# An encoder trunk whose start loads lie in one array: norm weights, first weight chunk and x side by side, and the small loads on SyncE's queue

## The chip, the cores and the metric

The kernel runs on one core of a Trainium2 chip. The metric is the device time of one execution in microseconds. The kernel before takes 593.35 us (median of 3 runs, 592.43 to 595.54). The engines are named as in the profile: PE (TensorE), DVE (VectorE), ACT (ScalarE), POOL (GpSimd) and SP (SyncE, which here only issues transfers).

## The reference, cut to what matters

Two residual layers over x of 256 tokens and 1024 features, all in float32:

```
h = x
for layer in range(2):
    hn = rms_norm(h, norm_mix_g[layer])
    if layer == 0:                       # grouped-query attention (A) beside dilated attention (B)
        qa, ka, va, qb, kb, vb = split(hn @ ab_w_in[0])
        qa, ka = rope(rms_norm(qa, a_q_norm_g)), rope(rms_norm(ka, a_k_norm_g))
        mix = concat(attention_A(qa, ka, va), attention_B(qb, kb, vb, rel_bias)) @ ab_w_out[0]
    else:                                # latent attention
        mix = mla_attention(hn, c_w_down, c_q_norm_g, c_kv_norm_g, c_w_uq, c_w_ukv) @ c_w_out
    h = h + mix
    hn = rms_norm(h, norm_mlp_g[layer])
    h = h + square(relu(hn @ mlp_w1[layer])) @ mlp_w2[layer]
return rms_norm(h, final_norm_g)
```

## The kernel before, in words

**Weights as a stream.** All weights lie in one array `wall`, cut into chunks of 128 rows by 2048 columns (1 MB each) in the order of their use. Chunks 0 and 1 (`qA`) make the queries of mixer A, chunk 2 (`kvA`) its keys and values, chunks 3 and 4 (`qkB` 0 and 1) the first half of the queries and of the keys of mixer B, chunks 5 and 6 their second half. `load` (L204) brings a chunk into one of three buffers `raw`; `split_piece` (L212) splits a quarter of it (later a half) into a rounded part `whi` (a copy on ACT, L222) and the remainder `wlo` (a subtraction on DVE, L223). When the last quarter of chunk i is split, `load(i + 3)` is given to SP (L225). Every product is three matmuls (`mm3`, L260): high by high (L263), high by low (L264), low by high (L265).

**The start.** PE runs 9 matmuls on zeros (L656). Chunk 0 comes in four quarters, each followed by rows of the transposed x (`xT`); the norm weights `g` (35 columns) come between. Then come chunk 1 in two halves, chunk 2 and the table `kc` with the identity, all issued by SP in this order. POOL issues three small loads: `gaq` (64 KB, one row of 512 bytes given to all 128 partitions, L645), `oh` (66 KB, L647) and `rb` (1 KB, L649). For each of the eight row blocks kk of x, `split_piece` prepares the weights, ACT scales xT by the norm weights and rounds it (hT, L663), DVE makes the remainder (L664), and PE does 6 matmuls of 512 columns. The code up to L677 is under `manual_schedule`: it stands in each engine's program as written.

**What follows.** 48 matmuls of 256 columns with chunk 2 (acckv), then 48 with chunk 3 and 48 with chunk 4 into the banks `s` (`qk_b(0)`, L781). Beside them `mixer_a` (L716) prepares mixer A: squares of the queries and keys on ACT (L720, L721), sums on DVE; the mean square of x (`mean_square`, L321: four squares of `xh` on ACT, L326); on POOL the tables `tab` and a chain of small operations that ends in `rs0`, the norm's factor by token (`rsqrt`, L307, L319); on DVE the rotation of the queries (`rope_a`, L696, result `qr`, last step L706), which PE then transposes (L752). `row_scales` (L332) multiplies the identity by `rs0` on DVE (`dg`, L336) for two more matmuls (L337). The scores of the first head (L847) close this stage.

**What sets the order.** From kvA on, a scheduler at build time decides the order of the instructions in each engine's program, from costs and arrival times that it assumes; the order of the code is only its input. Each engine then executes its own program strictly in that order. An instruction that waits holds up all that stand behind it on its engine.

Of the kernel before, what the change touches and what calls it, by code (L numbers as in the profile page):

```python
# [11 lines left out]
F32 = mybir.dt.float32  # L12
# [25 lines left out]
G_MIX, G_MLP, G_CQ, G_CKV = 0, 16, 32, 34  # L38
N_G = 35
R_AQ, R_AK, R_FIN = 0, 64, 128  # L40
N_R = 128 + D
# [4 lines left out]
def shape_constants():  # L46
    """Rotary tables, the relative-position buckets and the branch counts: of the shapes alone."""
    f = np.float32
# [44 lines left out]
def weight_chunks():  # L93
    """The order in which the weights stream in: (name, columns used)."""
    order = [("qA", 0), ("qA", 1), ("kvA", 0)]
    order += [("qkB", i) for i in range(4)] + [("vB", 0), ("vB", 1)]
    order += [("outA", i) for i in range(4)]
    for l in range(2):
        if l == 1:
            order += [("down", 0), ("down", 1), ("uq", 0), ("uq", 1), ("ukv", 0)]  # L100
            order += [("outC", i) for i in range(4)]
        for u in range(17):
            if u < 16:
                order.append((f"w1_{l}", u))
            if u > 0:
                order.append((f"w2_{l}", u - 1))
    return order
# [11 lines left out]
def pack_weights(ab_w_in, ab_w_out, c_w_down, c_w_uq, c_w_ukv, c_w_out, mlp_w1, mlp_w2):  # L119
    """All weights in the order of their use, each chunk as 128 partition rows."""  # L120
    win, wout = ab_w_in[0], ab_w_out[0]
# [44 lines left out]
@with_exitstack  # L166
def encoder(ctx: ExitStack, tc: tile.TileContext, x, xt, wall, gcol, grow, const, onehot, relb, out):
    nc = tc.nc
# [19 lines left out]
    def o_bank():  # L188
        return psum("o", 2)
# [9 lines left out]

# [1 line left out]
    raws, parts, done = {}, {}, set()  # L201
# [10 lines left out]
    def split_piece():  # L212
        """The next quarter of a chunk as two parts; of a chunk of the MLPs, the next half."""
        i, q = divmod(at["piece"], 4)
        n = 2 if i >= 5 else 1
        at["piece"] += n
        if q % 2 == 0:
            parts[i, q // 2] = [wp.tile([P, CW // 2], F32R, name=z, tag=z, bufs=W_BUFS) for z in ("whi", "wlo")]
        hi, lo = parts[i, q // 2]
        raw = raws[i][:, 512 * q:512 * (q + n)]  # L220
        s = slice(512 * (q % 2), 512 * (q % 2 + n))
        nc.scalar.copy(hi[:, s], raw)  # L222
        nc.vector.tensor_tensor(lo[:, s], raw, hi[:, s].bitcast(F32), op=OP.subtract)  # L223
        if q + n == 4:
            load(i + RAW_BUFS)  # L225
# [10 lines left out]
    def quarter(n=2):  # L236
        """A quarter of a chunk has been used."""
        at["quarter"] += 1
        pump(n)

    def take(name, j, n, whole=True):
        """A chunk of n row blocks: its operands by row block and columns."""
        i = at["take"]
        assert ORDER[i] == (name, j), (ORDER[i], name, j)
        at["take"] += 1
        while whole and at["piece"] < 4 * i + 4:
            split_piece()

        def operand(k, c=slice(None)):
            half, kk = divmod(k, n // 2)  # L250
            return tuple(z.rearrange("p (k c) -> p k c", k=n // 2)[:, kk, c] for z in parts[i, half])

        return i, operand
# [3 lines left out]
    def cols(i, n=P):  # L257
        return slice(i * n, i * n + n)

    def mm3(out, a, b, first, last):  # L260
        """out += a.T @ b, of operands that are each a sum of two parts."""
        (ah, al), (bh, bl) = a, b
        nc.tensor.matmul(out, ah, bh, start=first, stop=False)  # L263
        nc.tensor.matmul(out, ah, bl, start=False, stop=False)  # L264
        return nc.tensor.matmul(out, al, bh, start=False, stop=last)  # L265
# [6 lines left out]

# [1 line left out]
    g = cp.tile([P, N_G], F32, name="g")  # L274
# [4 lines left out]
    nc.vector.memset(idle, 0.0)  # L279
    xT = ap.tile([P, KT, S], F32, name="xT", tag="OT0")  # L280
    xt_v = xt.rearrange("(k p) t -> p k t", p=P)

    def load_x(a, b):
        nc.sync.dma_start(xT[:, a:b], xt_v[:, a:b])

    raws[0] = wp.tile([P, CW], F32, name="raw", tag="raw", bufs=RAW_BUFS)
    for a, b in ((0, 1), (1, 2), (2, 4), (4, 8)):
        for q in range(a, min(b, 4)):
            nc.sync.dma_start(raws[0][:, cols(q, 512)], wall[0, :, cols(q, 512)])
        load_x(a, b)  # L290
        if a == 0:
            nc.sync.dma_start(g, gcol)
    load(1, 2)
    load(2)
    kc = cp.tile([P, N_K], F32, name="kc")
    xh = cp.tile([P, NT, D], F32, name="xh")
    nc.sync.dma_start(kc, const)
    ident, flip = kc[:, K_ID:K_ID + P], kc[:, K_FLIP:K_FLIP + P]
    junk = cp.tile([P, 512], BF16, name="junk")
# [7 lines left out]
    def rsqrt(u, n, dst):  # L307
        """u ** -0.5, with one Newton step behind the power."""
        y, z = (small(16)[:, :n] for _ in range(2))
# [11 lines left out]
    def mean_square(name):  # L321
        """mean(h * h) + eps, a column for each token block."""
        part, u = small(4), cp.tile([P, NT], F32, name=f"u{name}")
        for t in range(NT):
            for c in range(2):
                nc.scalar.activation(junk, xh[:, t, cols(c, 512)], AF.Square,  # L326
                                     accum_out=part[:, 2 * c + t:2 * c + t + 1])
        nc.gpsimd.tensor_tensor(u, part[:, 0:2], part[:, 2:4], op=OP.add)
        nc.gpsimd.tensor_scalar(u, u, 1.0 / D, EPS, op0=OP.mult, op1=OP.add)
        return u  # L330

    def row_scales(bank, which, columns):  # L332
        """Values by token, spread over all partitions with the tokens along the row."""
        for t in range(NT):
# [3 lines left out]

# [1 line left out]
    def attention(heads, fill, dst):  # L340
# [34 lines left out]
        def values(j):  # L375
            """The weighted values of a pair of heads, side by side in the array."""
            ob = o_bank()
# [34 lines left out]
    def scaled_softmax(scale, nscale):  # L412
        """exp(scale * (s - max)) and its sums, the scale by query."""
        nb = {}
# [21 lines left out]
    def turn(c, t, gbase):  # L436
        """Half a token block of the residual stream, transposed, gained and split."""
        with tc.high_priority():
# [12 lines left out]
    class Later:  # L451
        """The turn of the last group, given out while the next one is computed."""
        todo = None
# [170 lines left out]

# [1 line left out]
    with tc.tile_pool(name="l0", bufs=1) as lp:  # L626
# [17 lines left out]

        nc.gpsimd.dma_start(gaq, bass.AP(tensor=grow.tensor, offset=grow.offset, ap=[[0, P], [1, P]]))  # L645
        oh = sp.tile([P, 512], F32, name="oh", tag="prob", bufs=3)
        nc.gpsimd.dma_start(oh[:NUM_BUCKETS + 1, :], onehot)  # L647
        nc.vector.memset(rb, 1.0)
        nc.gpsimd.dma_start(rb[:NUM_BUCKETS, :], relb)  # L649

        # q, then k and v, of mixer A
        acc = [mm_bank() for _ in range(NT)]
        with tc.manual_schedule():
# [3 lines left out]
            for j in range(2):  # L657
                i, w = take("qA", j, 4, whole=False)
                for k in range(4):
                    kk = 4 * j + k  # L660
                    gc = g[:, G_MIX + kk:G_MIX + kk + 1]
                    split_piece()
                    nc.scalar.activation(hT[0][:, kk], xT[:, kk], AF.Copy, scale=gc)  # L663
                    nc.vector.scalar_tensor_tensor(hT[1][:, kk], xT[:, kk], gc, hT[0][:, kk].bitcast(F32),  # L664
                                                   op0=OP.mult, op1=OP.subtract)
# [4 lines left out]
                if j == 0:  # L670
                    nc.sync.dma_start(xh, x.rearrange("(t p) d -> p t d", p=P))
            lines = o_bank()
            nc.tensor.matmul(lines[:HB, :], rb, oh[:NUM_BUCKETS + 1, :], start=True, stop=True)
# [16 lines left out]
        def load_bias(j):  # L690
            """rel_bias by distance, with the branch counts; query rows run backwards."""
            bias[j] = lp.tile([P, 2, 3 * P], F32, name="bias", tag="bias", bufs=2)
# [15 lines left out]
        def stack(dst, src, col):  # L708
            """Rows of two heads, each as its high part beside its low part in the other rows."""
            for s in range(2):  # L710
# [211 lines left out]

# [1 line left out]
    with tc.tile_pool(name="l1", bufs=1) as lp:  # L924
# [194 lines left out]
```

## Time and profile before

| what | before |
|---|---|
| runs, median (lowest to highest) | 593.35 us (592.43 to 595.54) |
| span of the profiled execution | 591.9 us |
| PE busy | 578.0 us (98%) |
| DVE, ACT, POOL busy | 364.7, 324.1, 35.0 us |
| first matmul on data | 6.21 us after the span's start |
| weights and inputs read | 95.05 MB |

The profiled execution has no time of its own beside its span; the span is 1.45 us below the median of the runs, and what lies around it is taken as these 1.45 us. PE is busy nearly all the time, so that time can be won or lost where PE stands idle or runs at the lower of its two clocks: at the start, in the stage up to 60 us, and at the end.

### The profile page before, as it was taken

What the parts mean: (1) busy time and instruction counts of PE and PEld (TensorE: products, weight loads), DVE (VectorE), ACT (ScalarE), POOL (GpSimd) and SP (SyncE); (2) the same over time, 40 slices, a digit from 0 to 9 for tenths busy, and PEclk for the clock granted to TensorE, in tenths of its full rate; (3) what the DMA queues carried; (4) which work ended last, traced back from release to release, by engine and by line L of the source; (5) the groups of instructions that cost most, each with busy time, mean ns of one, the idle gap of its engine ahead of it and who ended that gap; (6) DMA issues with size and microseconds to landing.
All of it is one profiled execution on the core that took longest, in us unless ns stands there. A gap on an engine that the chain in (4) does not pass through costs nothing.

```text
span 591.9 us, 8924 instructions
## 1 busy us (share of the span) xinstructions
PE 578.0 (98%) x3553; PEld 493.9 (83%) x3553; DVE 364.7 (62%) x583; ACT 324.1 (55%) x550; POOL 35.0 (6%) x70
## 2 busy tenths in 40 slices
PE   7989999999999999999999999999999999999994
PEld 3889665689998998898889987779899889989984
DVE  4888776586545546555468888757555645555425
ACT  5768875564444444435447498836444444544414
POOL 1480000000000000000002200000000000000003
PEclk9989999999999999999999999999999999999998
DMA  8955133135454555545544323146454554554201
GB/s 277 406 200 214 71 137 131 73 142 187 170 205 163 201 174 186 210 157 200 195 161 163 123 73 142 35 145 204 159 206 158 198 206 155 209 181 174 73 1 71
DMA packets 16602, 96.69 MB, mean 163 GB/s; under 512 B 1922, under 2 KB 3970, under 8 KB 5808
## 3 DMA queue, kind: packets, MB, share of 16 engines
q1 hardware_dynamic: 15984, 94.92, 43.9%
q0 software_dynamic: 288, 0.68, 0.5%
q8 instruction: 28, 0.46, 0.3%
q10 hardware_dynamic: 288, 0.52, 0.2%
q14 instruction: 14, 0.11, 0.1%
HBM read 95.05 MB, written 1.06 MB: 162 GB/s over the span
## 4 chain that ended last, share of the span: by engine, by line
PE 88%; ACT 3%; DMA 3%; DVE 2%; POOL 2%; issue 1%; SPq 1%; POOLq 0%; DVEq 0%; ACTq 0%
PE mm L263 15%; PE mm L264 15%; PE mm L265 14%; PE s L263 10%; PE s L264 10%; PE s L265 10%; PE o L380 3%; DMA raw<-in_wall 3%; PE o L391 3%; PE s L1075 2%; PE s L848 2%; PE s L847 1%; PE o L441 1%; DVE wlo L223 1%; ACT whi L222 1%
## 5 line engine op out<-in xcount | busy, mean ns | idle before, releaser
L223 DVE TENSOR_TENSOR wlo<-raw,whi 128x1024 fp32r<-128x1024 f32 (+1 forms) x182 | 208.9, 1165 | 150.3 <-ACT whi L222 150.1
L222 ACT CAST whi<-raw 128x1024 fp32r<-128x1024 f32 (+1 forms) x182 | 178.4, 1002 | 155.2 <-issue 66.3
L263 PE MATMUL s<-hT,whi 128*128 128x256 f32 x512 | 145.6, 284 | 0.0
L264 PE MATMUL s<-hT,whi 128*128 128x256 f32 x512 | 145.4, 284 | 0.0
L265 PE MATMUL s<-hT,wlo 128*128 128x256 f32 x512 | 145.2, 284 | 0.0
L264 PE MATMUL mm<-wlo,h2h 128*128 128x512 f32 x252 | 100.5, 399 | 0.0
L263 PE MATMUL mm<-whi,h2h 128*128 128x512 f32 x252 | 99.7, 396 | 0.0
L263 PEld LDWEIGHTS s<-hT,whi 128*128 128x128 f32 x512 | 98.4, 192 | 1.5
L264 PEld LDWEIGHTS s<-hT,whi 128*128 128x128 f32 x512 | 98.4, 192 | 1.3
L265 PEld LDWEIGHTS s<-hT,wlo 128*128 128x128 f32 x512 | 98.4, 192 | 0.1
L265 PE MATMUL mm<-whi,h2l 128*128 128x512 f32 x252 | 98.3, 393 | 0.0
L265 PEld LDWEIGHTS mm<-whi,h2l 128*128 128x128 f32 x252 | 47.3, 188 | 11.5 <-DVE h2l L514 0.4
L263 PEld LDWEIGHTS mm<-whi,h2h 128*128 128x128 f32 x252 | 47.4, 188 | 11.2 <-ACT h2h L513 0.7
L264 PEld LDWEIGHTS mm<-wlo,h2h 128*128 128x128 f32 x252 | 47.3, 188 | 9.5
L513 ACT CAST h2h<-work 128x512 fp32r<-128x512 f32 x32 | 19.9, 621 | 42.0 <-DVE work L510 42.0
L514 DVE TENSOR_TENSOR h2l<-work,h2h 128x512 fp32r<-128x512 f32 x32 | 22.2, 692 | 20.6 <-ACT h2h L513 20.6
L263 PE MATMUL mm<-whi,OT 128*128 128x512 f32 x64 | 26.9, 421 | 0.0
L510 DVE TENSOR_TENSOR work<-work 128x512 f32<-128x512 f32 x32 | 21.9, 685 | 7.7 <-ACT work L509 7.7
L264 PE MATMUL mm<-wlo,OT 128*128 128x512 f32 x64 | 25.8, 406 | 0.0
L265 PE MATMUL mm<-whi,OT 128*128 128x512 f32 x64 | 25.4, 401 | 0.0
L263 PE MATMUL mm<-whi,hT 128*128 128x512 f32 (+1 forms) x64 | 23.0, 360 | 2.3 <-ACT hT L663 2.2
L394 ACT COPY pts<-o 128x512 f32<-128x512 f32 x32 | 18.7, 589 | 10.9 <-PE o L391 10.8
(229 smaller groups left out, 770.6 us busy)
## 6 DMA issues: line engine op xcount, KB each, us to landing
raw<-in_wall SPq DMA_DIRECT2D x84, 1024.0 KB, 4.8
bias<-line_d SPq DMA_DIRECT2D x4, 384.0 KB, 3.5
raw<-in_wall SPq DMA_DIRECT2D x4, 256.0 KB, 5.5
raw<-in_wall SPq DMA_DIRECT2D x2, 512.0 KB, 7.7
xh<-in_x SPq DMA_DIRECT2D x1, 1024.0 KB, 10.7
xT<-in_xt SPq DMA_DIRECT2D x1, 512.0 KB, 6.9
kc<-in_const SPq DMA_DIRECT2D x1, 512.0 KB, 9.8
grw<-in_grow POOLq DMA_DIRECT2D x1, 512.0 KB, 4.8
```

The lines of the kernel that those rows point to most:

```text
L222: nc.scalar.copy(hi[:, s], raw)
L223: nc.vector.tensor_tensor(lo[:, s], raw, hi[:, s].bitcast(F32), op=OP.subtract)
L263: nc.tensor.matmul(out, ah, bh, start=first, stop=False)
L264: nc.tensor.matmul(out, ah, bl, start=False, stop=False)
L265: return nc.tensor.matmul(out, al, bh, start=False, stop=last)
L380: nc.tensor.matmul(ob[64 * s:64 * s + 64, :S], heads[2 * j + s]["v"](c), pts[2 * j + s][:, cols(c, S)], start=c == 0, stop=c == NT - 1)
L391: turned = nc.tensor.transpose(pt[:, c * S + q * P:c * S + q * P + P], prob[h][:, i, cols(c)], flip if flipped else ident)
L394: nc.scalar.copy(pts[h], pt)
L510: nc.vector.tensor_tensor(r, r, r, op=OP.mult)
L513: nc.scalar.copy(hi, halves(r))
L514: nc.vector.tensor_tensor(lo, halves(r), hi.bitcast(F32), op=OP.subtract)
L848: nc.tensor.matmul(o, q[s][own, j, cols(order[i])], kl, start=False, stop=True)
```

## The change

The host now lays an array `head` out: in each of 128 rows the norm weights (35 columns and one of padding), then four times 512 columns of chunk 0 with the 256 columns of x that go with them, then the other four blocks of x. It comes in five transfers: 804, 768, 768, 768 and 1024 columns. The first four land in two tiles `head0` and `head1`, the fifth in a tile `rest`, which takes one of the three `raw` buffers. `gaq`, `oh` and `rb` are issued by SP, behind `kc`. The norm weights are read out of `head0` at the start; POOL copies them into `g` for later. Since no chunk 0 is split out of a `raw` buffer, `load(3)` is no longer given when chunk 0 is done, but behind the eighth block, after `load(4)`, which the last split of chunk 1 gives. Lines of the changed kernel stand up to 9 higher than before.

```diff
+H_Q = (36, 804, 0, 768)
...
-        raw = raws[i][:, 512 * q:512 * (q + n)]
+        raw = head_w(q) if i == 0 else raws[i][:, 512 * q:512 * (q + n)]
...
-        if q + n == 4:
+        if q + n == 4 and i > 0:
             load(i + RAW_BUFS)
...
-    xT = ap.tile([P, KT, S], F32, name="xT", tag="OT0")
-    xt_v = xt.rearrange("(k p) t -> p k t", p=P)
-    def load_x(a, b):
-        nc.sync.dma_start(xT[:, a:b], xt_v[:, a:b])
-    raws[0] = wp.tile([P, CW], F32, name="raw", tag="raw", bufs=RAW_BUFS)
-    for a, b in ((0, 1), (1, 2), (2, 4), (4, 8)):
-        for q in range(a, min(b, 4)):
-            nc.sync.dma_start(raws[0][:, cols(q, 512)], wall[0, :, cols(q, 512)])
-        load_x(a, b)
-        if a == 0:
-            nc.sync.dma_start(g, gcol)
+    heads_ = [ap.tile([P, CW], F32, name=f"head{i}", tag=f"OT{i}") for i in range(2)]
+    rest = wp.tile([P, CW], F32, name="rest", tag="raw", bufs=RAW_BUFS)
+    def head_w(q):
+        return heads_[q // 2][:, H_Q[q]:H_Q[q] + 512]
+    def xT(k):
+        if k < 4:
+            return heads_[k // 2][:, H_Q[k] + 512:H_Q[k] + 512 + S]
+        return rest[:, cols(k - 4, S)]
+    at_col = 0
+    for q in range(4):
+        lo, hi = (0 if q == 0 else H_Q[q]), H_Q[q] + 512 + S
+        nc.sync.dma_start(heads_[q // 2][:, lo:hi], head[:, at_col:at_col + hi - lo])
+        at_col += hi - lo
+    nc.sync.dma_start(rest[:, :4 * S], head[:, at_col:at_col + 4 * S])
     load(1, 2)
     load(2)
...
     nc.sync.dma_start(kc, const)
+    nc.gpsimd.tensor_copy(g, heads_[0][:, :N_G])
...
-        nc.gpsimd.dma_start(gaq, bass.AP(tensor=grow.tensor, offset=grow.offset, ap=[[0, P], [1, P]]))
+        nc.sync.dma_start(gaq, bass.AP(tensor=grow.tensor, offset=grow.offset, ap=[[0, P], [1, P]]))
-        nc.gpsimd.dma_start(oh[:NUM_BUCKETS + 1, :], onehot)
+        nc.sync.dma_start(oh[:NUM_BUCKETS + 1, :], onehot)
-        nc.gpsimd.dma_start(rb[:NUM_BUCKETS, :], relb)
+        nc.sync.dma_start(rb[:NUM_BUCKETS, :], relb)
...
-                    gc = g[:, G_MIX + kk:G_MIX + kk + 1]
+                    gc = heads_[0][:, G_MIX + kk:G_MIX + kk + 1]
...
                 if j == 0:
                     nc.sync.dma_start(xh, x.rearrange("(t p) d -> p t d", p=P))
+                else:
+                    load(3)
```

The scheduler's answer changes with it. Three places follow, each before and now. On ACT, from the split of chunk 2 (the first four copies `whi`) on; `work<-mm` are the squares for mixer A, `junk<-xh` those of x. Before:

```order
L222 CAST whi<-raw 128x512 x4
L720 ACTIVATE work<-mm 128x512
L676 COPY ls<-o 8x512
L222 CAST whi<-raw 128x512 x4
L326 ACTIVATE junk,sm_401<-xh 128x512
L721 ACTIVATE work<-mm 128x128
L720 ACTIVATE work<-mm 128x512
L721 ACTIVATE work<-mm 128x128
L326 ACTIVATE junk,sm_401<-xh 128x512 x3
L222 CAST whi<-raw 128x512 x4
```

Now, on the same engine from the same place:

```order
L223 CAST whi<-raw 128x512 x4
L729 ACTIVATE work<-mm 128x512
L685 COPY ls<-o 8x512
L333 ACTIVATE junk,sm_399<-xh 128x512 x3
L730 ACTIVATE work<-mm 128x128
L729 ACTIVATE work<-mm 128x512
L730 ACTIVATE work<-mm 128x128
L333 ACTIVATE junk,sm_399<-xh 128x512
L223 CAST whi<-raw 128x512 x8
```

The four copies of chunk 3 moved behind the squares of the keys (`work<-mm 128x128`, which read acckv), and three of the four squares of x moved ahead of these. On DVE, from the split of chunk 3 on (`wlo`, the first row), before; the row behind the last one is `dg<-kc,rs`:

```order
L223 TENSOR_TENSOR wlo<-raw,whi 128x512 x4
L723 TENSOR_REDUCE sums<-work 128x2
L701 TENSOR_TENSOR kr<-mm,tab 128x128
L702 TENSOR_TENSOR work<-mm,tab 128x8x32
L722 TENSOR_REDUCE sums<-work 128x8
L723 TENSOR_REDUCE sums<-work 128x2
L704 TENSOR_TENSOR work<-mm,tab 128x8x32
L701 TENSOR_TENSOR qr<-mm,tab 128x512
L706 TENSOR_TENSOR qr<-qr,work 128x512
L223 TENSOR_TENSOR wlo<-raw,whi 128x512 x4
L702 TENSOR_TENSOR work<-mm,tab 128x8x32
L704 TENSOR_TENSOR work<-mm,tab 128x8x32
```

Now, on DVE from the second of these rows on; the eight `wlo` at the end are chunks 3 and 4:

```order
L710 TENSOR_TENSOR kr<-mm,tab 128x128
L711 TENSOR_TENSOR work<-mm,tab 128x8x32
L731 TENSOR_REDUCE sums<-work 128x8
L732 TENSOR_REDUCE sums<-work 128x2
L713 TENSOR_TENSOR work<-mm,tab 128x8x32
L710 TENSOR_TENSOR qr<-mm,tab 128x512
L715 TENSOR_TENSOR qr<-qr,work 128x512
L711 TENSOR_TENSOR work<-mm,tab 128x8x32
L713 TENSOR_TENSOR work<-mm,tab 128x8x32
L343 TENSOR_SCALAR dg<-kc,rs_119 128x128
L715 TENSOR_TENSOR qr<-qr,work 128x512
L224 TENSOR_TENSOR wlo<-raw,whi 128x512 x8
```

The subtractions of chunks 3 and 4 moved behind `dg`, which reads `rs0`, and behind the rotated queries of the second token block. On PE, from the last matmuls with chunk 2 (bank `mm`) to the first with chunk 3 (bank `s`), before:

```order
L263 MATMUL mm<-whi,hT_102 128x256
L264 MATMUL mm<-wlo,hT_102 128x256
L265 MATMUL mm<-whi,hT_103 128x256
L263 MATMUL s<-whi,hT_102 128x256
L264 MATMUL s<-wlo,hT_102 128x256
```

Now:

```order
L264 MATMUL mm<-whi,hT_100 128x256
L265 MATMUL mm<-wlo,hT_100 128x256
L266 MATMUL mm<-whi,hT_101 128x256
L761 MATMUL o<-kc,qr 128x128 x4
L264 MATMUL s<-whi,hT_100 128x256
L761 MATMUL o<-kc,qr 128x128 x3
L265 MATMUL s<-wlo,hT_100 128x256
```

The transposes of the rotated queries, of the first token block (four) and of the second (three of four), moved ahead of the matmuls with chunk 3. Elsewhere on PE, `L682` (the bias line, L673 before) moved behind the first 13 matmuls with chunk 2. From the second product of the attention's output projection on, the programs of all engines are the same.

## Rows read from the trace of the kernel before

**Rows 1.** The page: the span, and each engine's busy time.
```profile
span 591.9 us, 8924 instructions
PE 578.0 (98%) x3553; PEld 493.9 (83%) x3553; DVE 364.7 (62%) x583; ACT 324.1 (55%) x550; POOL 35.0 (6%) x70
```
**Rows 2.** Timeline of PE, the eight blocks: start us, us, engine line op [idle before].
```profile
6.21 0.50 PE L263 MATMUL mm<-whi,hT 128*128 128x512 f32 x1 [1.33 <-ACT hT L663]
...
13.92 0.50 PE L263 MATMUL mm<-whi,hT 128*128 128x512 f32 x1 [0.16 <-ACT hT L663]
...
19.51 0.39 PE L265 MATMUL mm<-whi,hT 128*128 128x512 f32 x1
```
**Rows 3.** Timeline of ACT at the start.
```profile
3.88 0.62 ACT L222 CAST whi<-raw 128x512 fp32r<-128x512 f32 x1 [1.67 <-DMA raw<-in_wall]
5.65 0.51 ACT L663 ACTIVATE hT<-xT,g 128x256 fp32r<-128x256 f32 x1 [1.15 <-DMA g<-in_gcol]
...
12.84 0.62 ACT L222 CAST whi<-raw 128x512 fp32r<-128x512 f32 x1 [1.32 <-DMA raw<-in_wall]
```
**Rows 4.** Windows: us, busy by engine, PE's granted clock, DMA share, GB/s.
```profile
2.00:3.00 1.00, 1.00 (x4) 0.41 (x3) 0.00 (x0) 0.21 (x2) 0.99 (x3) 1.00 0.57 197
4.00:5.00 1.00, 0.88 (x3) 0.15 (x1) 0.46 (x1) 0.50 (x1) 0.00 (x0) 1.00 0.75 123
5.00:6.00 1.00, 0.00 (x0) 0.00 (x0) 0.23 (x1) 0.35 (x1) 0.00 (x0) 1.00 0.75 133
...
8.00:10.00 2.00, 1.33 (x5) 0.91 (x6) 1.74 (x3) 1.23 (x3) 0.00 (x0) 1.00 1.07 365
```
**Rows 5.** DMA queues from 2 to 4 us: packets, MB, share of 16 engines.
```profile
q1 hardware_dynamic: 320, 0.37, 54.9%
q0 software_dynamic: 22, 0.07, 31.4%
```
**Rows 6.** Timeline of ACT around the end of the matmuls with chunk 2.
```profile
26.46 0.28 ACT L721 ACTIVATE work<-mm 128x128 f32<-128x128 f32 x1 [2.29 <-PE mm L265]
...
27.79 0.21 ACT L326 ACTIVATION_READ_ACCUMULATOR junk<-xh 128x1 f32 x1
...
29.33 0.19 ACT L326 ACTIVATION_READ_ACCUMULATOR junk<-xh 128x1 f32 x1
```
**Rows 7.** Timeline of POOL: first and last step of the chain to rs0.
```profile
29.60 0.36 POOL L328 TENSOR_TENSOR ua<-sm 128x2 f32<-128x2 f32 x1 [5.50 <-ACT junk L326]
...
34.96 0.19 POOL L319 TENSOR_TENSOR rs<-sm,sm 128x2 f32<-128x2 f32 x1
```
**Rows 8.** Timeline of DVE: rotated queries of both token blocks, and dg between.
```profile
29.22 0.68 DVE L706 TENSOR_TENSOR qr<-qr,work 128x512 f32<-128x512 f32 x1
...
35.19 0.28 DVE L336 TENSOR_SCALAR dg<-kc,rs 128x128 f32<-128x128 f32 x1 [1.94 <-POOL rs L319]
...
37.35 0.69 DVE L706 TENSOR_TENSOR qr<-qr,work 128x512 f32<-128x512 f32 x1
```
**Rows 9.** Timeline of PE from chunk 3 to the first scores.
```profile
26.62 0.28 PE L263 MATMUL s<-whi,hT 128*128 128x256 f32 x1
...
35.94 0.28 PE L265 MATMUL s<-hT,wlo 128*128 128x256 f32 x1
38.10 0.76 PE L752 MATMUL o<-kc,qr 128*128 128x128 f32 x4 [1.89 <-DVE qr L706]
...
43.08 0.60 PE L809 MATMUL s<-kc,work 128*128 128x128 f32 x4
...
53.19 0.38 PE L847 MATMUL s<-kdA,qA 128*128 128x256 f32 x1
```
**Rows 10.** Windows around that wait: PE's granted clock is third from the end.
```profile
38.00:39.00 1.00, 0.90 (x6) 0.90 (x7) 0.94 (x4) 1.00 (x1) 1.00 (x6) 0.76 0.00 0
39.00:40.00 1.00, 1.00 (x7) 1.00 (x6) 1.00 (x1) 0.98 (x3) 1.00 (x1) 0.50 0.00 0
...
42.00:43.00 1.00, 1.00 (x11) 1.00 (x10) 0.97 (x2) 0.00 (x0) 0.91 (x3) 1.00 0.87 369
```

More of the change, by code (lines that the diff above doesn't have):

```diff
@@ L166, in encoder @@
 @with_exitstack
-def encoder(ctx: ExitStack, tc: tile.TileContext, x, xt, wall, gcol, grow, const, onehot, relb, out):
+def encoder(ctx: ExitStack, tc: tile.TileContext, x, head, wall, grow, const, onehot, relb, out):
     nc = tc.nc
@@ L660, in encoder @@
                     kk = 4 * j + k
-                    gc = g[:, G_MIX + kk:G_MIX + kk + 1]
+                    gc = heads_[0][:, G_MIX + kk:G_MIX + kk + 1]
                     split_piece()
-                    nc.scalar.activation(hT[0][:, kk], xT[:, kk], AF.Copy, scale=gc)
-                    nc.vector.scalar_tensor_tensor(hT[1][:, kk], xT[:, kk], gc, hT[0][:, kk].bitcast(F32),
+                    nc.scalar.activation(hT[0][:, kk], xT(kk), AF.Copy, scale=gc)
+                    nc.vector.scalar_tensor_tensor(hT[1][:, kk], xT(kk), gc, hT[0][:, kk].bitcast(F32),
                                                    op0=OP.mult, op1=OP.subtract)
@@ L1099 @@
         "x": np.ascontiguousarray(a["x"][0]),
-        "xt": np.ascontiguousarray(a["x"][0].T),
+        "head": None,
         "wall": pack_weights(a["ab_w_in"], a["ab_w_out"], a["c_w_down"], a["c_w_uq"], a["c_w_ukv"],
                              a["c_w_out"], a["mlp_w1"], a["mlp_w2"]),
-        "gcol": np.ascontiguousarray(np.concatenate(
-            [column(a["norm_mix_g"]), column(a["norm_mlp_g"]), column(a["c_q_norm_g"]),
-             column(a["c_kv_norm_g"])], 1)),
         "grow": np.concatenate([a["a_q_norm_g"][0], a["a_k_norm_g"][0], a["final_norm_g"]])[None],
@@ L1110 @@
     }
+    xt = a["x"][0].T.reshape(KT, P, S)
+    gains = np.concatenate([column(a["norm_mix_g"]), column(a["norm_mlp_g"]), column(a["c_q_norm_g"]),
+                            column(a["c_kv_norm_g"]), np.zeros((P, 1), np.float32)], 1)
+    first = arrays["wall"][0].reshape(P, 4, 512)
+    arrays["head"] = np.ascontiguousarray(np.concatenate(
+        [gains] + [z for k in range(4) for z in (first[:, k], xt[k])] + [xt[k] for k in range(4, 8)], 1))
     nc = bacc.Bacc("TRN2", target_bir_lowering=False, num_devices=1)
```

## The prediction

> **What bounds the kernel now.** I read the page first: PE is busy 98% of 591.9 us [rows 1], so the reader looks for stretches where PE waits or runs slowly. The waits by engine name two places, and the timeline shows them. At the start the first matmul on data stands at 6.21 us and the 48th begins at 19.51 us [rows 2]. Of these 13.3 us some 11 are matmuls; the rest is waiting for hT and, behind that, for transfers: ACT waits 1.15 us for the norm weights although the first quarter of chunk 0 came at 3.88, and again 1.32 us until the first half of chunk 1 lands at 12.84 [rows 3]. The windows say why the transfers are late: 197, 123 and 133 GB/s in three windows between 2 and 6 us, 365 GB/s between 8 and 10 [rows 4]. In 2 to 4 us POOL's queue takes 31.4% of the 16 engines for 0.07 MB, SP's queue 54.9% for 0.37 MB [rows 5].
>
> The second place is behind chunk 2. PE goes from chunk 2 to chunk 3 without a gap at 26.62 us, stops after 35.94 us for 1.89 us, waiting for the rotated queries, and then runs at half clock for some 3.5 us [rows 9, 10]. From 43.08 us on (the transposes L809) it is busy up to the tail. The wait hangs on a chain: the last square of x ends at 29.52 us, POOL needs until 35.15 us for `rs0`, and DVE's `dg` starts at 35.19 us after 1.94 us of idling for it [rows 6 to 8]. Before, this long chain lay beside 75 matmuls with chunks 3 and 4.
>
> **First part: the transfers of the start (gain).** Up to the first half of chunk 1 there were to come, before, chunk 0 and x (1.05 MB each), 0.02 MB of norm weights, 0.13 MB of POOL's loads and that half (0.52 MB), 2.77 MB; now 2.64 MB. From 2 to 6 us about 0.7 MB moved (0.44 in 2 to 4 [rows 5], 0.12 and 0.13 in the next two [rows 4]); at 365 GB/s it would be 1.46 MB. I take it that POOL's loads are the brake, since the slow windows are those in which its queue holds engines. Then 0.76 MB come earlier, worth 2.1 us, and 0.13 MB need not come, worth 0.35 us, 2.4 us at best; I take 2.3, since the very first transfers ramp up in any case. So the first half of chunk 1 lands at 10.5 us. From its landing to the first matmul that uses it takes 1.08 us (12.84 to 13.92), and block 4 starts at 11.6 us, if the blocks before are done. They are: the first transfer brings 0.41 MB where 0.26 MB had landed at 3.88 us, so it lands 0.4 us later, at 4.3 us, and block 0 starts 1.08 us behind, near 5.4; matmuls of this part follow each other every 0.24 us (13.92 to 19.51 is 23 of them), so four blocks of six take 5.8 us. The 48th matmul begins at 17.2 us: **−2.3 us**. Bounds: if only the 0.13 MB are saved, −0.35 us; if no block waits for data and block 0 starts when the zeros' matmuls end (PE busy 0.88 us from 4 to 5 us and not at all from 5 to 6 [rows 4]), the 48th comes 47 × 0.243 us behind 4.9 us, at 16.3 us, −3.2 us.
>
> [...]
>
> **Second part: the small loads behind `kc`, the copy of `g`, the later loads.** `oh` and `rb` are needed by L682, now behind 13 matmuls with chunk 2, near 19 us. The other half of chunk 1, chunk 2, `kc` and the small loads are 2.2 MB and take 6.1 us behind the 10.5: they land near 16.6 us, and xh by 19.5, when its squares on ACT begin at about 20 us, behind L682's copy. Chunk 4, then chunk 3, are requested near 16 us, when the eighth block is split, and come behind xh at 2.9 us each, near 22.4 and 25.3 us; ACT reads chunk 3 at 25.7 us (below). So all of it is hidden, chunk 3 narrowly; were it 1 us late, the subtractions would not be, since they wait longer for other things. The copy of `g` on an idle POOL costs nothing.
>
> **Third part: the order behind chunk 2 (cost).** Let E be the end of chunk 2's matmuls: 26.62 us before, 24.3 us now (17.2 and the same 7.1 us). Each step is counted from E. ACT: the copies of chunk 3 now stand behind four instructions that wait for acckv. They start at E − 0.16 as before (26.46); the last of them, a square of x, ends at E + 1.38 (28.00, when the second square ended before [rows 6]); before, all four squares were done at E + 2.90. POOL's chain and `dg` follow by 5.67 us (29.52 to 35.19; one of its steps now stands behind `rs0`, 0.15 us): `dg` at E + 6.9. DVE: the other products are done by E + 4 (two short ones behind the first `qr`, E + 3.3), then it idles until `dg`. Behind `dg` come `qr` of the second block (0.7 us) and the first `wlo` of chunk 3 (0.69 us): E + 8.4. PE: it waits for `qr` of the first block (E + 3.3; 29.22 + 0.68 before), does four transposes and one matmul, waits for `qr` of the second block (E + 7.8), does three transposes, and can go on with chunk 3 only at **E + 8.4**. Before, it went on at E.
>
> From there the same work is left: 47 matmuls with chunk 3, 48 with chunk 4, a transpose and the two `dg` matmuls, up to L809's counterpart. At full clock a matmul costs 0.12 us (the 74 matmuls and 4 transposes from 26.62 to 35.94 take 9.32 us), so 5.6 + 5.8 + 0.5 = 11.9 us. PE will have been idle for nearly all of 8 us. [...] A `wlo` of DVE takes 0.69 us (as `qr`, of the same size, in rows 8) and is good for six matmuls, 0.72 us, so DVE doesn't limit. L809's counterpart comes at E + 8.4 + 11.9 + 1.75 = E + 22.05, before at E + 16.46 (43.08): **+5.6 us**. Bounds: no half clock at all, +3.8 us; half clock twice as long, +7.3 us.
>
> Up to the first scores ACT has the same list as before, about 10 us behind L809 (53.19 − 43.08), but PE reaches them 4 matmuls sooner in its program and waits for them: **+0.4 us** (0 to 0.8). Past that PE was full and the work is the same.
>
> **The sum** is −2.3 + 5.6 + 0.4 = +3.7 us: the span goes from 591.9 to 595.6 us, and the time, with the 1.45 us by which the runs' median lies above the span, from 593.35 to 597.05 us.
>
> **The rivals.**
> *The transfers gain all that they can, or PE's clock does not fall, or both.* −3.2 + 5.6 + 0.4 = +2.8, −2.3 + 3.8 + 0.4 = +1.9, both together +1.0 us: about 595.3 us. For it: POOL's queue holds a third of the engines for a sixth of the bytes [rows 5]. Against it: the clock fell after a far shorter wait.
> *The brake was not POOL's queue.* The slow windows are the ramp of the first transfers and come again; then only 0.13 MB are saved, and the sum is −0.35 + 5.6 + 0.4 = +5.65 us: 599.0 us. For it: the window of 2 to 3 us is slow too, when transfers have barely begun. Against it: 4 to 6 us is slower still. [...]
> *Not slower: the chain to `rs0` is over before PE needs it.* The place is DVE's wait at `dg`. If `rs0` were done by E, the stall would shrink to the copies of chunk 3, and −2.3 us stands nearly alone: 591.05 us. It decides from the point where the last square of x ends 7 us before E, but this square now stands behind the squares of acckv, which can't start before E − 0.16.
>
> **Chances and range.** The forecast, 595.7 to 598.5 us, 55%; the first rival 25%; the second 15%; the last 5%. This kernel's measurement can tell about 0.5%, 2.97 us, from no change. Over 596.3 us lie the second rival and most of the forecast (about 48 of 55) with little of the first: 0.64 slower. The first rival, the low end of the forecast and most of the last are within 0.5%: 0.32. Faster by more needs the last rival with the full gain of the start: 0.04. The range 594.0 to 600.0 us leaves out the last rival, the lowest of the first and the highest of the second.
>
> **What would show each step.** Chunk 1's first copy on ACT near 10.5 us, and windows between 3 and 6 us near 350 GB/s; the 48th matmul near 17.2 us; no wait at L682; PE idle for nearly 8 us behind chunk 2, the releasers DVE `qr` and then `wlo`; DVE idle before `dg` by some 3 us for POOL's `rs0`; `dg` 6.9 us behind the end of chunk 2; a granted clock of 0.5 after it; L809's counterpart near 46.4 us in place of 43.08; the first scores near 57 us; the rest of the programs shifted by the same 3.7 us. The prediction is wrong if PE goes on with chunk 3 sooner than 6 us behind chunk 2, or if the start gains over 4 us.

## The result, and the profile after

The changed kernel takes 599.94 us (median of 6 runs, 599.53 to 600.74), the kernel before 593.18 us (6 runs beside it, 592.43 to 595.54): a ratio of 1.0105, 95% interval 1.0087 to 1.0124. It is slower, by 2.9 us more than forecast. The page has the span at 597.6 us, 5.7 us longer than [rows 1], with the same 3553 matmuls:

```profile
span 597.6 us, 8922 instructions
PE 581.0 (97%) x3553; PEld 495.2 (83%) x3553; DVE 364.8 (61%) x583; ACT 324.1 (54%) x550; POOL 31.8 (5%) x68
```

**The start.** PE's timeline: the first matmul on data, the first of block 4 and the 48th (start us, us, engine, line, operation, idle before).

```profile
5.09 0.54 PE L264 MATMUL mm<-whi,hT 128*128 128x512 f32 x1
...
11.71 0.51 PE L264 MATMUL mm<-whi,hT 128*128 128x512 f32 x1 [0.50 <-ACT hT L670]
...
17.32 0.39 PE L266 MATMUL mm<-whi,hT 128*128 128x512 f32 x1
```

ACT at the start: the first quarter's copy, hT right behind it, and the first copy of chunk 1.

```profile
4.01 0.62 ACT L223 CAST whi<-head 128x512 fp32r<-128x512 f32 x1 [1.79 <-DMA head<-in_head]
4.53 0.51 ACT L670 ACTIVATE hT<-head 128x256 fp32r<-128x256 f32 x1
...
10.63 0.62 ACT L223 CAST whi<-raw 128x512 fp32r<-128x512 f32 x1 [1.71 <-DMA raw<-in_wall]
```

The windows of the start, GB/s last:

```profile
2.00:3.00 1.00, 1.00 (x4) 0.41 (x3) 0.00 (x0) 0.21 (x2) 0.00 (x0) 1.00 0.72 241
4.00:5.00 1.00, 1.00 (x3) 0.15 (x1) 0.34 (x1) 0.99 (x2) 0.21 (x1) 1.00 0.92 323
5.00:6.00 1.00, 1.00 (x4) 0.61 (x4) 0.83 (x3) 0.77 (x3) 0.00 (x0) 1.00 1.04 353
```

The wait for norm weights is gone, 4 to 6 us moves 323 and 353 GB/s in place of 123 and 133 [rows 4, 5], and the 48th matmul begins 2.19 us sooner [rows 2, 3].

**Behind chunk 2.** ACT's timeline, its last square of x and its copies of chunks 3 and 4:

```profile
25.61 0.21 ACT L333 ACTIVATION_READ_ACCUMULATOR junk<-xh 128x1 f32 x1
26.23 4.25 ACT L223 CAST whi<-raw 128x512 fp32r<-128x512 f32 x8 [0.41 <-DMA raw<-in_wall]
```

POOL's timeline, its last step to `rs0`:

```profile
30.05 0.19 POOL L326 TENSOR_TENSOR rs<-sm,sm 128x2 f32<-128x2 f32 x1
```

DVE's timeline, the rotated queries of both token blocks, `dg`, and the subtractions of chunk 3:

```profile
27.04 0.68 DVE L715 TENSOR_TENSOR qr<-qr,work 128x512 f32<-128x512 f32 x1
...
30.27 0.28 DVE L343 TENSOR_SCALAR dg<-kc,rs 128x128 f32<-128x128 f32 x1 [1.89 <-POOL rs L326]
30.48 0.68 DVE L715 TENSOR_TENSOR qr<-qr,work 128x512 f32<-128x512 f32 x1
31.08 2.50 DVE L224 TENSOR_TENSOR wlo<-raw,whi 128x512 fp32r<-128x512 f32 x4
```

PE's timeline, from the last matmul with chunk 2 to the first scores:

```profile
24.32 0.28 PE L266 MATMUL mm<-whi,hT 128*128 128x256 f32 x1
27.78 0.66 PE L761 MATMUL o<-kc,qr 128*128 128x128 f32 x4 [3.18 <-DVE qr L715]
...
31.22 0.90 PE L761 MATMUL o<-kc,qr 128*128 128x128 f32 x3 [2.66 <-DVE qr L715]
31.82 0.58 PE L265 MATMUL s<-wlo,hT 128*128 128x256 f32 x1
...
45.65 0.60 PE L818 MATMUL s<-kc,work 128*128 128x128 f32 x4
...
56.24 0.38 PE L856 MATMUL s<-kdA,qA 128*128 128x256 f32 x1 [0.36 <-ACT kdA L787]
```

The reader sees the chain of the prediction: DVE stands before `dg` until POOL has `rs0`, 1.89 us, the subtractions of chunk 3 stand behind (begun at 31.08 us, though ACT's first copy of it ended at 26.84), and PE goes on with chunk 3 only 7.4 us behind the end of chunk 2 (E, 24.44: the last start, 24.32, and the 0.12 us from one matmul to the next), where before there was no gap [rows 6 to 9]. The granted clock (third from the end) fell from 1.00 to 0.50 while PE stood idle (0.55 on average from 29 to 30 us) and stays at 0.50 until about 36 us, as behind the shorter wait in [rows 10]; in windows of 0.1 us the traces of both kernels show 1.00 or 0.50, and other values only where it changes:

```profile
30.00:32.00 2.00, 0.78 (x4) 0.69 (x5) 1.73 (x4) 2.00 (x4) 2.00 (x5) 0.50 0.54 197
34.00:36.00 2.00, 2.00 (x12) 2.00 (x12) 1.99 (x4) 0.00 (x0) 2.00 (x4) 0.52 0.51 152
36.00:38.00 2.00, 2.00 (x19) 2.00 (x18) 1.92 (x3) 0.58 (x1) 2.00 (x4) 1.00 1.05 442
```

**Behind the first scores**, where nothing was expected, more is lost while PE shows hardly a wait. The same place of the program, before and after:

| PE begins | before | after | later by |
|---|---|---|---|
| 48th matmul | 19.51 | 17.32 | −2.19 |
| L809 / L818 | 43.08 | 45.65 | +2.57 |
| first scores | 53.19 | 56.24 | +3.05 |
| second product of the output projection | 133.63 | 139.91 | +6.28 |
| `dg` matmuls of layer 1 | 333.24 | 339.36 | +6.12 |

From the first scores to the output projection PE does the same instructions in 80.4 us before and 83.7 us after. Summed by operation, each from its start to that of the next, the value matmuls (L380, now L387) take 11.1 us before and 13.1 after, the transposes of the probabilities (L391, L398) 6.8 and 7.6, all others within 0.4. The value matmuls write two heads into the two halves of one bank (64 of its 128 partitions each; 128*64 in the rows), and the order of PE's program differs. After, three of them in a row, then one alone; each shows as two records (32 for the 16 that read `vA`), so x6 is three matmuls:

```profile
79.92 1.08 PE L387 MATMUL o<-pts,vA 128*64 128x256 f32 x6
80.92 0.55 PE L398 MATMUL o<-kc,prob 128*128 128x128 f32 x3
...
82.14 0.65 PE L387 MATMUL o<-pts,vA 128*64 128x256 f32 x2
82.72 0.38 PE L857 MATMUL s<-klA,qA 64*128 64x256 f32 x1
```

After, elsewhere, two in a row:

```profile
73.92 0.65 PE L387 MATMUL o<-pts,vA 128*64 128x256 f32 x4
74.50 0.38 PE L856 MATMUL s<-kdA,qA 128*128 128x256 f32 x1
```

The kernel before, four in a row:

```profile
75.45 1.08 PE L380 MATMUL o<-pts,vA 128*64 128x256 f32 x8
76.47 0.50 PE L264 MATMUL mm<-wlo,hT 128*128 128x512 f32 x1
```

From start to next start: one 0.58 us, two 0.58, three 1.00, four 1.02. One alone costs as much as two neighbours. The records of two neighbours lie side by side: those at 73.92 us in the rows above begin 0.01 us apart and take 0.43 us each, the next two, 0.27 us later, again 0.01 us apart. The two programs place the 32 value matmuls of this layer so:

| | fours | threes | twos | alone | sum by these prices |
|---|---|---|---|---|---|
| before | 4 | 3 | 0 | 7 | 11.1 us |
| after | 2 | 3 | 1 | 13 | 13.2 us |

These prices allow an estimate of what is lost. A place for one matmul or for two neighbours costs about 0.43 us (three or four less two), and each group 0.15 us more. Before there are 21 places in 14 groups, after 24 in 19. So of the 2.0 us some 1.3 are neighbours pulled apart, and some 0.7 is the larger number of groups; no run sets these two apart.

### The profile page after: what moved, and what is told of

Its sections match the earlier page's. It is cut to its first block, busy times and chain, and to the rows that moved or that the text cites. A ratio compares the mean times of both kernels' runs of the same rounds, so it can differ in the third digit from the quotient of the medians.

```text
span 597.6 us, 8922 instructions
## 1 busy us (share of the span) xinstructions
PE 581.0 (97%) x3553; PEld 495.2 (83%) x3553; DVE 364.8 (61%) x583; ACT 324.1 (54%) x550; POOL 31.8 (5%) x68
## 4 chain that ended last, share of the span: by engine, by line
PE 90%; ACT 4%; DVE 2%; POOL 2%; DMA 1%; issue 1%; SPq 0%; POOLq 0%; DVEq 0%; ACTq 0%
PE mm L265 15%; PE mm L264 15%; PE mm L266 15%; PE s L265 10%; PE s L264 10%; PE s L266 10%; PE o L387 4%; PE o L398 3%; PE s L1084 2%; PE s L857 2%; DMA raw<-in_wall 1%; PE s L856 1%; PE o L448 1%; ACT whi L223 1%; POOL sm L322 1%
## 5 line engine op out<-in xcount | busy, mean ns | idle before, releaser
L224 DVE TENSOR_TENSOR wlo<-raw,whi 128x1024 fp32r<-128x1024 f32 (+1 forms) x178 | 205.7, 1174 | 146.5 <-ACT whi L223 146.2
L223 ACT CAST whi<-raw 128x1024 fp32r<-128x1024 f32 (+1 forms) x178 | 175.8, 1011 | 152.2 <-issue 63.5
L264 PEld LDWEIGHTS s<-hT,whi 128*128 128x128 f32 x512 | 97.9, 191 | 1.5
L265 PEld LDWEIGHTS s<-hT,whi 128*128 128x128 f32 x512 | 97.9, 191 | 1.2
```

## The experiments

Three things can be set apart: the layout of `head`, the queue of the small loads, and the time at which `load(3)` is given. The scheduler's order hangs on the last two alone: with the layout undone or done, PE's program comes out the same. So the layout's effect can be had at an unchanged order, and two kernels (e3, e6) change the order of the attention alone (that of layer 1 too, where the value matmuls stand in 7 fours, 1 three and 1 alone in all four kernels, 8.7 us).

**e1: `load(3)` early again.**

```diff
-    rest = wp.tile([P, CW], F32, name="rest", tag="raw", bufs=RAW_BUFS)
+    rests = [sp.tile([P, 512], F32, name="rest", tag="pts", bufs=3) for _ in range(2)]
...
-        if q + n == 4 and i > 0:
+        if q + n == 4:
             load(i + RAW_BUFS)
...
-                else:
-                    load(3)
```

> The changed kernel with the last four blocks of x in two small buffers of their own, so that all three raw buffers hold weights and the load of chunk 3 is given, as before, when chunk 0 is split. The subtractions of chunk 3 then stand ahead of dg again. Theory 1 (the loss is the order: the late split of chunk 3, 3.05 us net of the start by the first scores, and singly placed value matmuls in the attention): start -2.2 us; no wait before chunk 3; its program has 10 value matmuls standing alone, 4 twos, 2 threes, 2 fours, by 0.58, 0.6, 1.0 and 1.02 us 12.2 us in place of 11.1, +1.1 us; dg stands ahead of the subtractions of chunk 4, which may cost up to 1.6 us more than before. Sum -1.1 to +0.5: 592.1 to 593.7 us. Theory 2 (the loss comes with the transfers themselves, small loads on SyncE's queue and pieces of head): it stays, 598 to 600 us.

Measured: 594.35 us (ratio to before 1.0009, 0.9995 to 1.0022), span 591.8. PE goes from chunk 2 to 3 without a gap and waits later, for chunk 4's subtractions, which now stand behind `dg` (PE's timeline, that wait and the first scores):

```profile
33.45 0.39 PE L266 MATMUL s<-hT,wlo 128*128 128x256 f32 x1 [2.49 <-DVE wlo L224]
...
51.43 0.39 PE L855 MATMUL s<-kdA,qA 128*128 128x256 f32 x1
```

The first scores come 1.76 us sooner than before. Of after's loss 5.6 us are gone with all its transfers kept: theory 2 falls. The median is 0.65 us over the range given. Against the kernel before as it ran beside e1 (593.90 us) it is +0.45, within the sum of −1.1 to +0.5: the median span of e1's 12 runs is 592.4 us, 0.3 over that of before's 29, and what lies outside the span is 0.2 us longer.

**e2: the layout alone** (e1 with the three loads on GpSimd's queue).

```diff
-        nc.sync.dma_start(gaq, ...); nc.sync.dma_start(oh[...]); nc.sync.dma_start(rb[...])
+        nc.gpsimd.dma_start(gaq, ...); nc.gpsimd.dma_start(oh[...]); nc.gpsimd.dma_start(rb[...])
```

> As e1, and the three small loads on GpSimd's queue again. PE's program is then instruction for instruction that of the kernel before; what differs is the layout of the first transfers alone. Theory 1 (GpSimd's queue is the brake of the start): the windows between 3 and 6 us stay near 130 GB/s, the 48th matmul comes only by the 0.13 MB earlier, -0.35 us: 592.8 us. Theory 2 (the layout takes the brake away: five large transfers for nine, no wait for g): -2.2 us: 591.0 us.

Measured: 593.46 us (0.9990, 0.9973 to 1.0007). One window of the start:

```profile
5.00:6.00 1.00, 1.00 (x3) 0.69 (x3) 0.83 (x2) 0.43 (x2) 0.00 (x0) 1.00 1.11 81
```

ACT's first copy of chunk 1:

```profile
12.86 0.62 ACT L223 CAST whi<-raw 128x512 fp32r<-128x512 f32 x1 [1.70 <-DMA raw<-in_wall]
```

The slump is there and chunk 1 comes as late as before (12.84): the layout alone gains nothing at the start. Theory 1 holds here.

**e4: the layout undone, the rest as after.**

```diff
-        nc.gpsimd.dma_start(gaq, ...); nc.gpsimd.dma_start(oh[...]); nc.gpsimd.dma_start(rb[...])
+        nc.sync.dma_start(gaq, ...); nc.sync.dma_start(oh[...]); nc.sync.dma_start(rb[...])
...
-        if q + n == 4:
+        if q + n == 4 and i > 0:
...
                     nc.sync.dma_start(xh, x.rearrange("(t p) d -> p t d", p=P))
+                else:
+                    load(3)
```

> The kernel before with the small loads on SyncE's queue and the load of chunk 3 given late; the layout of the first transfers is the old one. PE's program is instruction for instruction that of the changed kernel. If GpSimd's queue was the brake of the start, nearly all of the gain of the start is here too (but for 0.13 MB, 0.35 us): 600.3 us, the 48th matmul at 17.7. If the layout was it, the start is that of the kernel before, 48th matmul at 19.5: 602.1 us.

Measured: 602.67 us (1.0142, 1.0121 to 1.0164). Two windows of the start:

```profile
4.00:5.00 1.00, 1.00 (x3) 0.15 (x1) 0.18 (x1) 0.83 (x2) 0.00 (x0) 1.00 0.85 228
5.00:6.00 1.00, 0.96 (x3) 0.61 (x3) 0.91 (x2) 0.22 (x1) 0.00 (x0) 1.00 0.95 207
```

ACT's first copy of chunk 1:

```profile
13.20 0.62 ACT L222 CAST whi<-raw 128x512 fp32r<-128x512 f32 x1 [1.48 <-DMA raw<-in_wall]
```

Without any load on GpSimd's queue the old layout still moves only 207 to 228 GB/s, and chunk 1 lands no sooner than before. My reading, that GpSimd's loads were *the* brake, falls: there are two, either of which is enough.

**e9 to e12: which brakes.** All four are the changed kernel with one edit at the start.

```diff
 e9:  each of the four transfers of head cut in two, weights (2 KB a row) and x (1 KB a row)
 e10: head[:, 0:36] (the norm weights) as a transfer of its own, rows of 144 bytes
 e11: -nc.sync.dma_start(gaq, ...)   +nc.gpsimd.dma_start(gaq, ...)
 e12: -nc.sync.dma_start(oh, rb ...) +nc.gpsimd.dma_start(oh, rb ...)
```

> The changed kernel with each of the first four transfers cut in two, the weights (2 KB a row, the first with the norm weights 2.2 KB) and the x that goes with them (1 KB a row): the same bytes from the same array in 9 transfers. The programs are those of the changed kernel. e4 moved 185 to 238 GB/s between 2 and 6 us with such rows and no loads on GpSimd's queue. If rows of 1 and 2 KB are what slows it: about 230 GB/s here too, the first half of chunk 1 at about 12.8 us, 602 us. If it was the separate norm weights, in rows of 140 bytes: 320 to 350 GB/s as in the changed kernel, 10.6 us, 599.9 us.

> The changed kernel with the norm weights in a transfer of their own (rows of 144 bytes) ahead of the first weights. The programs are those of the changed kernel. If short rows in general are the brake of e4, this small transfer costs at most 0.3 us, first half of chunk 1 at 10.6 to 10.9 us. If the norm weights' rows were what slowed e4: about 230 GB/s and 12.5 us or later.

> The changed kernel with one of the small loads, gaq (one row of 512 bytes given to all 128 partitions), on GpSimd's queue again; oh and rb stay on SyncE's. A few instructions change places behind chunk 2; what is read is the start. In e2, with all three on GpSimd's queue, the window of 5 to 6 us fell to 81 GB/s and the first half of chunk 1 landed at 12.86 us. If it is the transfer to all partitions that brakes: the same slump, 12 us or later. If it is oh (33 rows of 2 KB): no slump, 10.7 us.

> The counterpart of e11: oh and rb on GpSimd's queue, gaq on SyncE's. If gaq alone brakes: no slump, first half of chunk 1 at 10.7 us. If any load on GpSimd's queue does, since its packets hold the engines for longer: a slump of about half the size, 11.5 to 12 us; if it is oh: 12.8 us.

ACT's first copy of chunk 1 in e9:

```profile
11.98 0.62 ACT L223 CAST whi<-raw 128x512 fp32r<-128x512 f32 x1 [2.64 <-DMA raw<-in_wall]
```

In e10:

```profile
11.36 0.62 ACT L223 CAST whi<-raw 128x512 fp32r<-128x512 f32 x1 [2.09 <-DMA raw<-in_wall]
```

In e11:

```profile
12.30 0.62 ACT L223 CAST whi<-raw 128x512 fp32r<-128x512 f32 x1 [1.50 <-DMA raw<-in_wall]
```

In e12:

```profile
11.32 0.62 ACT L223 CAST whi<-raw 128x512 fp32r<-128x512 f32 x1 [1.94 <-DMA raw<-in_wall]
```

GpSimd's queue from 4 to 6 us in e11:

```profile
q0 software_dynamic: 16, 0.06, 67.2%
```

In e12:

```profile
q0 software_dynamic: 51, 0.06, 9.8%
```

GB/s in e11 while these packets are under way:

```profile
6.00:7.00 1.00, 1.00 (x6) 0.85 (x5) 0.68 (x2) 0.70 (x2) 0.00 (x0) 1.00 0.36 94
```

Against 10.63 us in the changed kernel, e9 is 1.35 us late, e10 0.73, more than I gave it, e11 1.67 and e12 0.69. In e1, e3, e5, e7 and e8, whose start is that of the changed kernel or nearly so, the same copy begins at 10.59 to 10.85 us, so these figures are good to about 0.2 us.

Two brakes show in the rate. Short rows: e9 moves 241 and 268 GB/s between 4 and 6 us in place of 323 and 353, with the engines as busy (98.6% of 16 engines for 0.51 MB, 97.9% for 0.68 MB in the changed kernel); so it is not that they wait for the issue of more transfers. And `gaq`, given to GpSimd's queue ahead of all: its 16 packets of 4 KB are under way for 67.2% of 16 engines for 2 us, 1.34 us a packet, beside SP's 70.6% (137.8% together: packets of the two queues overlap). GB/s falls to 204 and 94 from 5 to 7 us, where the changed kernel moves 353 and 330. The same bytes of `oh` take 9.8%, and e12 moves 370 GB/s in each us from 4 to 7.

So e12's 0.69 us are no slump, and what they are stays open. Nor is e10's loss one: with the norm weights ahead, 120 GB/s move from 2 to 3 us in place of 241, then 378 and 369 from 4 to 6.

Whether GpSimd's queue or the place ahead of the weights makes `gaq` a brake is not set apart. The changed kernel has it on SP's queue behind `kc` (issued at 5.26, landed at 17.46 us), and while it, `oh` and `rb` are under way, the rate falls there too; no wait of PE's follows:

```profile
15.00:16.00 1.00, 1.00 (x6) 0.80 (x6) 1.00 (x3) 1.00 (x4) 0.00 (x0) 1.00 0.37 129
```

The times of the four (601.39, 601.18, 598.30, 597.17 us) are not compared further, since e11 and e12 have other orders and e9 and e10 only two runs each.

**e3 and e6: the value matmuls tied.** e3 is the changed kernel, e6 the kernel before, each with

```diff
+            with tc.high_priority(100):
                 for c in range(NT):
                     for s in range(2):
                         nc.tensor.matmul(ob[64 * s:64 * s + 64, :S], ...)
```

> The changed kernel, with the four value matmuls of a pair of heads given a high priority, so that the scheduler puts them one behind the other (7 fours, 1 three, 1 alone in place of 2 fours, 3 threes, 1 two, 13 alone). Up to the scores its programs are those of the changed kernel. Theory 1 (value matmuls of two heads run side by side in the array only as neighbours; one alone takes 0.58 us, four together 1.02): 8.7 us in place of 13.2, -4.4 us: 595.5 us, a little more if what waits for other work eats some. Theory 2 (PE is full there and the same work takes the same time in any order; the 2.6 us behind the first scores have another cause): 599.9 us within 0.5.

> The kernel before with nothing but the value matmuls tied. It had 4 fours, 3 threes and 7 alone, 11.1 us; tied it has 7 fours, 1 three, 1 alone, 8.7 us. Theory 1 (neighbours run side by side): -2.4 us, 591.0 us. Theory 2 (what e3 won was a slot that only the changed order had lost): within 0.5 us of the kernel before, 593.4 us.

Measured: e3 595.19 us (594.68 to 595.67), 4.75 below the changed kernel, ratio to before 1.0012 (0.9999 to 1.0025) where that had 1.0105; e6 591.03 us, ratio to before 0.9964 (0.9945 to 0.9984). By the prices of the records 4.4 and 2.4 were expected; 4.75 and 2.6 came. The other theory falls in both.

In the profiles, the stage from the first scores to the second product of the output projection takes 79.7 us in e3 in place of 83.7, and 77.9 in e6 in place of 80.4: 4.0 and 2.5 us, with 8.7 us of value matmuls in both. Another 0.6 us of e3's lies ahead of the first scores (55.61 us in place of 56.24), where its programs are those of the changed kernel; from what it comes is not shown.

**e5 and e7: towards a better kernel.** e5 is e1 tied. e7 is the changed kernel, tied, with chunk 3 requested ahead of chunk 4:

```diff
-        if q + n == 4 and i > 0:
+        if q + n == 4 and i > 1:
             load(i + RAW_BUFS)
...
                 else:
                     load(3)
+                    load(4)
```

> e1 with the value matmuls tied as in e3 (7 fours, 1 three, 1 alone). If the parts add up: start -2.2 us, stage behind chunk 2 +0.5 (in e1 the first scores came 1.76 us sooner than before although chunk 2 ended 2.25 us sooner), value matmuls 8.7 us in place of before's 11.1, -2.4: -4.1 us, 589.3 us, and 5 us below e1 only where ties cost nothing elsewhere (e1's 12.2 less 8.7 is 3.5 us). If the parts don't add, since work that the scheduler had put between the value matmuls is then late: 592 us or more.

> The changed kernel with the load of chunk 3 ahead of that of chunk 4 (both requested behind the eighth block), and the value matmuls tied. The subtractions of chunk 3 stand ahead of the rotated queries again, but behind eight short DVE instructions that wait for chunk 2's matmuls, the squares of x ahead of those of the keys. If the order of DVE's program is what held PE: PE goes on with chunk 3 about 3.4 us behind the end of chunk 2 (7.2 in the changed kernel, 0 before), and needs no second wait; at half clock for some time 1 to 2 us. Start -2.2, stage +0.4 to +1.5, value matmuls -2.4: 589.2 to 590.3 us. If chunk 3's late arrival is what holds PE (it lands some 25 us after the span's start however it is ordered): no sooner than 6 us behind chunk 2, 593 us or more.

Measured: e5 590.90 us (0.9951, 0.9933 to 0.9969), 3.45 below e1, as the records say (12.1 less 8.7 us), but 1.6 over the 589.3 of parts that all add up and 1.1 under the 592 of parts that don't; e7 589.31 us (0.9917, 0.9893 to 0.9941), 5.9 below e3, from which it differs in the order of two loads. In e7 the subtractions of chunk 3 wait on DVE for nothing but the short work ahead of them. PE idles for 1.78 and 0.37 us, by its timeline:

```profile
26.56 0.42 PE L264 MATMUL s<-whi,hT 128*128 128x256 f32 x1 [1.78 <-ACT whi L223]
27.35 0.58 PE L265 MATMUL s<-wlo,hT 128*128 128x256 f32 x1 [0.37 <-DVE wlo L224]
```

DVE's timeline in e7:

```profile
26.62 2.48 DVE L224 TENSOR_TENSOR wlo<-raw,whi 128x512 fp32r<-128x512 f32 x4
```

Chunk 3's data come hardly sooner for it: ACT begins to copy them at 25.88 us, in the changed kernel at 26.23, while the subtractions begin at 26.62 and at 31.08. So the stall of the changed kernel was the order that the late request gave the programs, not the data's arrival. e7 beats both kernels, by 0.8% and 1.8%.

**e8: rows on multiples of 256 bytes.** A row of `head` has 16,528 bytes in the changed kernel, and most of its pieces begin off such multiples; whether that costs time here is what e8 shows.

```diff
-H_Q = (36, 804, 0, 768)
+H_Q = (64, 832, 0, 768)
```

> The changed kernel with 64 columns in place of 36 ahead of the first weights, so that rows of head are 16,640 bytes, a multiple of 256, and each piece begins on such a multiple. The programs are those of the changed kernel. [...]

ACT's first copy of chunk 1:

```profile
10.81 0.62 ACT L223 CAST whi<-raw 128x512 fp32r<-128x512 f32 x1 [1.90 <-DMA raw<-in_wall]
```

600.15 us, chunk 1 no sooner than 10.63: no gain from it here. The 0.18 us by which it is later are within what profiles of the same start differ by (10.59 to 10.85).

## Why the prediction was right in sign and 2.9 us short

The range ended at 600.0 us, 0.06 above the measured 599.94: that it held is luck. The time lies above the forecast's 595.7 to 598.5 us, and above the 599.0 of the second rival, whose reason, slow windows that come again, did not occur. What brought it there are 3.2 us in the attention that stood in no term; 0.8 us too much in the third part hid some of them.

**First part, the start: right in size, wrong in cause.** −2.3 us for the 48th matmul, −2.19 measured; first half of chunk 1 at 10.5 us, 10.63 measured. But "I take it that POOL's loads are the brake" is half of it: e2 and e4 show that taking away one of the two, the short rows of the old layout or the loads on GpSimd's queue, gives nothing. I had read the queues from 2 to 4 us only [rows 5]. From 4 to 6 us, in the two slowest windows of [rows 4], they stand so in the kernel before:

```profile
q1 hardware_dynamic: 207, 0.21, 59.0%
q0 software_dynamic: 29, 0.04, 16.3%
```

After, in the same window:

```profile
q1 hardware_dynamic: 250, 0.68, 97.9%
```

GpSimd's queue holds only 16.3% there before, and SP's takes 59.0% for 0.21 MB; by after's figures 0.21 MB would take about 30%. So a second brake could be seen, and 118 of that window's 236 packets were under 512 B, after 30 of 250. The second rival, that the slow windows come again, is excluded by after's windows.

**Second part: right.** No wait at L682, and the late chunk 3 was hidden: it landed near 26.2 us in place of 25.3, and ACT waited 0.41 us for it, while DVE stood at `dg` until 30.27.

**Third part, the order behind chunk 2: right in mechanism, 0.8 us too large.** Every step stands in the trace: PE's two waits for `qr` (3.18 and 2.66 us), `dg` behind `rs0` (1.89 us), a granted clock of 0.50 after it. For that clock the sum has 1.75 us, half of the 3.5 us at 0.50 behind the wait before [rows 10] (3.4 by windows of 0.1 us); after, the 20 matmuls from 31.82 to 35.99 us take 4.17 us at 0.50, mostly one every 0.21 us, 1.8 us more than at the 0.12 us each of full clock. The term that was too large is POOL's chain from the last square to `dg`: 4.4 us in place of the 5.67 of before, so PE went on at E + 7.4, not 8.4. Three of its steps ran shorter (0.22, 0.73 and 0.28 us in place of 0.54, 1.03 and 0.66); why is not shown. From E to the first scores the changed kernel is 5.2 us slower; 5.6 + 0.4 was predicted. e1 and e7, where that order is undone with the transfers kept, confirm it.

**The step that failed: "Past that PE was full and the work is the same."** The work is the same and PE was full, but not at the same pace: 3.2 us more from the first scores to the output projection, 2.0 of it by the value matmuls that the scheduler had pulled apart, 0.8 by transposes. I had looked at the orders behind chunk 2 and not at those of the attention, although they differ up to the output projection. e3 and e6 change that order alone and give 4.75 and 2.6 us back, 4.0 and 2.5 of them in that stage. The rows have the ground for it: two neighbours take 0.58 us, as one alone does, and their records begin 0.01 us apart; one alone has no such partner. Why the transposes cost 0.8 us more was not tried by itself; with the value matmuls tied, in e3, they take 7.0 us, so that most of it goes with that order.

**The sum.** −2.2 + 5.2 + 3.2 less 0.5 towards the end is the 5.7 us of the spans. The medians differ by 6.76 us, 1.1 more: each run of the changed kernel lies 1.8 to 2.1 us above its own span, mostly 2.0, each of before about 1.8 (+0.2; I had taken 1.45 for both, the median of the runs less the span of one); the six runs' median span is 597.95 us, 0.35 over the profiled one; and before's 593.18 less 1.8 is 591.4, 0.5 under its profiled span, which had the half clock (last section).

## What to carry to other kernels

Where a scheduler orders the programs, moving a transfer can reorder every engine behind it: compare the whole order, not the place of the edit, and count how often matmuls that take no longer as two neighbours than one takes alone (0.58 us here) are still neighbours. PE, with hardly a wait, lost 3.2 us, half a per cent, behind the first scores, 2.0 of it this way. At the start of a kernel look for every brake on the transfers: here they were short rows (1.35 us in e9) and a load to all partitions given to GpSimd's queue ahead of them (1.67 us in e11), and taking one away showed nothing (first copy of chunk 1 at 12.86 us in e2 and 13.20 in e4, 12.84 before).

## What the hardware showed that was not expected

A wait of 1.9 us was followed by a granted clock of 0.50 in the kernel before [rows 10], and not in e6. e6 has the programs of the kernel before up to there and waits 1.9 us for the rotated queries as well; its windows behind that wait, beside [rows 10] (PE alone, granted clock third from the end):

```profile
38.00:39.00 1.00, 0.70 (x6) 1.00 0.00 0
39.00:40.00 1.00, 0.99 (x9) 1.00 0.00 0
```

The granted clock stays at 1.00, and the transposes (L809, L810 in e6) begin at 41.98 us in place of 43.08 although chunk 2 ends 0.2 us later. Runs of the kernel before differ in the clock as well: of 29, eleven with spans of 590.9 to 591.3 us have a mean granted clock of 0.996 or 0.997, eleven with 593.6 to 594.1 have 0.987 to 0.991, and seven lie between. That it is this wait that parts them is not shown, since a run without a profile has only its mean clock. So a term for half clock was a chance here, not a fixed price: 1.1 us between these two profiles; between runs, whose spans differ by up to 3.2 us, it is not known.
